# MLA heads in pairs: V as the stationary operand of P times V, two heads in the two column halves

## The chip, the core and the metric

The kernel runs on one core of a Trainium2 chip. Its time is the device time in microseconds (us) of one execution. Each kernel was run several times; the median is given with the lowest and the highest. One execution more was taken with the hardware profiler on, and all rows of a profile come from that one. Engines are named as the profile names them: PE is TensorE's matmuls, PEld its weight loads, DVE VectorE, ACT ScalarE, POOL GpSimd, SP the queue that issues most of the loads.

## The reference: what is computed

One residual block on 512 positions of width 1024, in float32. The attention part, cut to what matters here:

```python
def mla_group(...):                      # 8 heads, 96 wide for q and k, 64 wide for v
    ...
    def one_block(args):
        ...
        logits = jnp.einsum('bhqd,bhkd->bhqk', qb, k_t).astype(jnp.float32) * scale
        logits = jnp.where(allowed[None, None], logits, NEG_INF)
        probs = jax.nn.softmax(logits, axis=-1).astype(v_t.dtype)
        return jnp.einsum('bhqk,bhkd->bhqd', probs, v_t)
    ...

# in reference():
x = x + jnp.concatenate([y_mla, y_diff], axis=-1) @ w_out[i]
x = x + conv_ffn(rms_norm(x, ffn_norm_g[i]), w_gate[i], w_up[i], conv_w[i], conv_b[i], w_down[i])
gate = jax.nn.sigmoid(rms_norm(x, ple_norm_g[i]) @ w_ple_gate[i])
x = x + gate * (p[i] @ w_ple_proj[i])
```

y_diff are four differential heads (two softmaxes each, subtracted, v 128 wide, an RMS norm behind). The mask lets a query see the keys of its own chunk of 64 positions and of all chunks before it.

## The kernel before, in words

Positions lie in four tiles of 128 (t = 0 to 3). Because of the mask a query tile t needs only the keys of tiles 0 to t, so everything of slot t has n = (t+1)·128 columns. Products whose error would matter are made of three matmuls of split operands (`mm3`, lines 157 to 159: high x high, high x low, low x high, in the type fp32r); a split is a cast on ACT (`S.copy`, the high half) and a subtraction on DVE (the low half). Transposes and P times V are plain f32.

In the order of time: the input projections of the latents; the q, k and v of the MLA heads; the eight MLA heads, with the projections of the differential heads (`zd`) as filling; the four differential heads, with the output projection (`o`) as filling; the feed-forward part; the last gate. PE's order is that of the code (`manual_schedule`). For DVE, ACT and POOL the code's order holds up to the `region.__exit__` inside the MLA loop; after it a scheduler orders them when the program is built, within hints such as `tc.issue_after`.

The MLA loop of before runs over 32 slots (h, t). For each:

- `mla_logits(h, t)`, one slot ahead: the logits into a bank `ml` (three matmuls), their row maximum times the query's scale (`nm`, DVE lines 572 and 573), then Exp on ACT into `pm`, with the row sums as a by-product.
- in the slots t < 2 of most heads, `mla_q` or `mla_k` of the next head: four transposes of 96 columns into a bank (`qT`, `kT`) and a split into `st`.
- `pump(n)`: n filling units, of six matmuls of 512 columns each. `FILL_MLA` gives n for t = 0 to 3.
- `probs_T`: t+1 transposes of `pm` into a bank `pT`, and a copy to `pt`, on DVE or ACT by t.
- `mla_pv`, one slot behind: `po[queries, 64] += pt^T · V`, with P as the stationary operand and 64 columns of V moving. After the last slot of a pair of heads one DVE operation scales the bank `mo` by the reciprocal of the sums into `ym` (lines 588 to 590).

The outcome has queries on the partitions. The output projection wants it the other way, so `y_split` transposes each `ym` (four transposes, `yT`) and splits the outcome into `yh` and `yl`. `zd_norm` scales the differential heads' q and k (`zd`) by their RMS on DVE: eleven small steps and four multiplications of 512 columns; it is called at two places in the MLA heads.

Banks of PSUM rotate by tag: two `acc` for filling, three `lg` for logits, two `tp` for transposes (`qT`, `kT`, `pT`), one `ob` for P times V. `pm` has four buffers, `pt` two.

Of the kernel before, what the change touches and what calls it, by code (L numbers as in the profile page):

```python
# [94 lines left out]
def hybrid_block(ctx: ExitStack, tc: tile.TileContext, a: dict, out: bass.AP):  # L95
# [15 lines left out]
    def bank(tag, name):  # L111
        return pp_.tile([P, 512], F32, tag=tag, bufs={"acc": 2, "lg": 3, "tp": 2, "ob": 1}[tag], name=name)
# [7 lines left out]
    def pm_tile(name):  # L120
        return att.tile([P, T], F32, tag="pm", bufs=PM, name=name)
# [10 lines left out]
    def th_tile(name):  # L132
        return wts.tile([P, T], F32R, tag="th", bufs=8, name=name), wts.tile([P, T], F32R, tag="tl", bufs=8, name=name + "l")
# [20 lines left out]
    def mm3(ps, blocks, first=True, last=True, again=False):  # L154
        n = len(blocks)
        for i, (xh, xl, wh, wl) in enumerate(blocks):
            TE.matmul(ps, xh, wh, start=first and i == 0, stop=False, skip_group_check=again)  # L157
            TE.matmul(ps, xh, wl, start=False, stop=False, skip_group_check=again)  # L158
            TE.matmul(ps, xl, wh, start=False, stop=last and i == n - 1, skip_group_check=again)  # L159
# [22 lines left out]
    def split(h_, l_, src, col=None, eng=None):  # L182

        if col is None:
            S.copy(h_, src)  # L185
            return (eng or V).tensor_tensor(l_, src, _f32(h_), op=ALU.subtract)
        else:
            S.activation(h_, src, AF.Identity, scale=col)
            return V.scalar_tensor_tensor(l_, src, col, _f32(h_), op0=ALU.mult, op1=ALU.subtract)
# [342 lines left out]
    pump(FILL_QK)  # L532


    def probs_T(pm, t, name, on_act):

        ps = bank("tp", f"pT{name}")
        n = (t + 1) * P
        for j in range(t + 1):
            TE.transpose(ps[:, tsl[j]], pm[:, tsl[j]], ident)  # L540
# [20 lines left out]

    mla, ymn = {}, []

    def mla_logits(h, t):
        qh_, ql_, kh_, kl_ = QT[h % 2]
        n = (t + 1) * P
        if h % 2 == 0 and t == 0:
            mla["ssum", h // 2] = sm.tile([P, NT, 2], F32, tag="ssum", name="ssum")
        ps = bank("lg", f"ml{h}{t}")
        mm3(ps[:, :n], [(qh_[:100, tsl[t]], ql_[:100, tsl[t]], kh_[:100, :n], kl_[:100, :n])])  # L570
        nm, r = sm.tile([P, 1], F32, tag="nm", bufs=4, name="nm"), rq[:, 0, t, h:h + 1]
        V.reduce_max(nm, ps[:, :n], axis=AX.X, negate=True)  # L572
        mla["nm"] = V.tensor_tensor(nm, nm, r, op=ALU.mult)  # L573
        pm = pm_tile("pm")
        S.activation(pm[:, :n], ps[:, :n], AF.Exp, bias=nm, scale=r, accum_out=mla["ssum", h // 2][:, t, h % 2:h % 2 + 1])  # L575
        mla["pm", h, t] = pm

    def mla_pv(h, t):
        hp, c = divmod(h, 2)
        if c == 0 and t == 0:  # L580
            mla["po"] = bank("ob", f"mo{hp}")
        po, pt = mla["po"], mla.pop(("pt", h, t))
        w = slice(t * P + 64 * c, t * P + 64 * c + 64)
        for j in range(t + 1):
            TE.matmul(po[:, w], pt[:, tsl[j]], kv[j][:, h, 96:], start=j == 0, stop=j == t)  # L585
        if c == 1 and t == NT - 1:
            rcp = sm.tile([P, NT, 2], F32, tag="rcp", name="rcp")
            V.reciprocal(rcp, mla["ssum", hp])
# [26 lines left out]
    def y_split(i, src, col, tag):  # L615

        ps = bank(tag, f"yT{i}")
        for t in range(NT):
            TE.transpose(ps[:, tsl[t]], src[:, tsl[t]], ident)
        yh[i], yl[i] = th_tile(f"yh{i}")  # L620
        df["ysplit"] = split(yh[i], yl[i], ps, col)
# [20 lines left out]
    def wo_units(kq, dqs, nk):  # L642

        for dq in dqs:
            w = wo_w(kq, dq)
            if kq:
                wo2[dq] = w
            for b in (2 * dq, 2 * dq + 1):
                ps = bank("acc", f"o{kq}{b}")
                for k in range(0, nk, 2):  # L650
                    mm3(ps, wo_blocks(4 * kq + k, 4 * kq + k + 2, b, w), k == 0, k == nk - 2)
                    if k == nk - 2:
                        add_x(b, ps)
                    yield

    def diff_T(h, c):
        ps = bank("tp" if h else "acc", f"d{c}T{h}")
# [58 lines left out]
    def load_x():  # L716
# [4 lines left out]
    last_mla = [  # L721
        lambda: diff_T(0, 0),
        lambda: diff_T(0, 1),
        lambda: (y_split(0, ymn[0], None, "acc"), y_split(1, ymn[1], None, "lg"), load_x()),
        lambda: y_split(2, ymn[2], None, "acc"),
    ]
    slots = [(h, t) for h in range(H) for t in range(NT)]
    mla_q(0)
    pump()
    mla_k(0)  # L730
    pump(2)
    mla_logits(0, 0)
    lo(*z1_[1])
    for i, (h, t) in enumerate(slots):
        if i < 2:
            (mla_q, mla_k)[t](1)
        if i + 1 < len(slots):
            mla_logits(*slots[i + 1])
        if i == 4:
            region.__exit__(None, None, None)  # L740
            held = tc.issue_after(mla["nm"].ins)
            held.__enter__()
        if i == 8:
            held.__exit__(None, None, None)
            with tc.issue_after(mla["k"].ins):
                zd_norm(0)
        if 0 < h < H - 1 and t < 2:
            (mla_q, mla_k)[t](h + 1)
        if i == 1:
            lo(*z1_hi(3))  # L750
        if i in (9, 11, 13, 15):
            with tc.issue_after(mla["nm"].ins):
                zw2.append(load_w(a["w_d"][2, len(zw2)], 1024, f"d2{len(zw2)}"))
        if h < H - 1:
            pump(FILL_MLA[t])
        if i == 6:
            bias_strip()
        if h == H - 1:
            if t == 0:
                pump(100)  # L760
                fill.append(wo_units(0, range(4), 4))
            last_mla[t]()
            if t == NT - 1:
                raw = load_raw(a["w_out"][0, 0], 1024, "o00")
                hi_o, lo_o = (wts.tile([P, 1024], F32R, tag=i, bufs=NW, name=f"{i}_o00") for i in ("hi", "lo"))
                S.copy(hi_o, raw)
                with tc.issue_after(df["ysplit"].ins):
                    V.tensor_tensor(lo_o, raw, _f32(hi_o), op=ALU.subtract)
                wo_first[0, 0] = (hi_o, lo_o)
        mla["pt", h, t] = probs_T(mla.pop(("pm", h, t)), t, f"m{h}{t}", t % 2)  # L770
        if i:
            mla_pv(*slots[i - 1])
    diff_logits(0, 0)
    mla_pv(*slots[-1])
    diff_logits(0, 1)
    diff_T(1, 1)
    pump()
    y_split(3, ymn[3], None, "tp")
    for i, (h, t) in enumerate(dslots):
        if i + 2 < len(dslots):  # L780
            diff_logits(*dslots[i + 2])
        pump(FILL_DIFF[h][t])
        df["pt", h, t] = probs_T(df.pop(("pm", h, t)), t, f"d{h}{t}", True)
        if i:
            diff_pv(*dslots[i - 1])
        if h + 1 < DH and t == 0:
            diff_T(h + 1, 0)
        if h and t == 1:
            df["scaling"]()
        if t == 3 and h + 2 < DH:  # L790
            diff_T(h + 2, 1)
        if h and t == 2:
            y_split(4 + h - 1, df["y", h - 1], ocol, "tp")
        if h and t == 3:
            if h == 2:
                fill.append(wo_units(1, range(2), 2))
# [660 lines left out]
```

## Time and profile before

| what | value |
|---|---|
| median of 3 runs | 648.66 us (648.49 to 649.44) |
| the profiled execution's own time | 648.05 us |
| its span, first to last instruction | 646.3 us |
| PE busy | 637.7 us, 99% of the span |
| DVE busy | 480.9 us, 74% |
| ACT busy | 362.3 us, 56% |
| MLA heads in the trace | first logits at 67.5 us, output projection from 161.0 us |
| granted clock of TensorE | 0.999 |

A row of a group of instructions reads: line, engine, operation, output<-inputs, shapes, count, then busy us and mean ns of one, then the idle time of the engine just before them and what ended it. A row of the timeline begins with the start in us and the duration in us; rows of one kind in sequence are merged, with their count behind the x. A matmul's duration holds its way through the array, and the next one starts before its end; so what a matmul takes of PE is read from one start to the next. One f32 matmul (not fp32r, not a transpose) has two records. A row of waits has who waited, for whom, the sum in us, the times and the longest.

### The profile page before, as it was taken

How to read it: one execution, taken by the hardware profiler on the slowest of the kernel's cores; microseconds unless marked ns; L12 is line 12 of the kernel's file. 1: busy time of each engine (PE TensorE's matmuls, PEld its weight loads, DVE VectorE, ACT ScalarE, POOL GpSimd, SP SyncE). 2: the span in 40 equal slices, each digit the busy share in tenths (PEclk: the TensorE clock that was granted, in tenths of full speed). 3: DMA queues.
4: the chain of work that ended last, by engine and by line, in shares of the span. 5: the costliest groups of instructions: out<-in, count | busy, mean ns of one | idle time of the engine just before them, and what ended most of it. 6: DMA issues, size and time to landing. Idle time of an engine off the chain costs nothing.

```text
span 646.3 us, 10248 instructions
## 1 busy us (share of the span) xinstructions
PE 637.7 (99%) x3916; PEld 567.4 (88%) x3916; DVE 480.9 (74%) x870; ACT 362.3 (56%) x630; POOL 56.0 (9%) x92
## 2 busy tenths in 40 slices
PE   9999999999999999999999999999999999999997
PEld 9988888888787887889999999999999999988886
DVE  6889687646988767888876767677767676769844
ACT  7897666556676465657554555455454545537211
POOL 1510040000000121000100000000001000000000
PEclk9999999999999999999999999999999999999999
DMA  8241225130610428636774646464646463541121
GB/s 308 94 164 51 81 82 165 34 125 20 180 37 2 163 87 255 163 66 180 191 216 114 180 115 187 120 195 119 181 114 180 115 180 115 180 131 52 39 89 50
DMA packets 29912, 82.63 MB, mean 128 GB/s; under 512 B 3100, under 2 KB 4124, under 8 KB 29736
## 3 DMA queue, kind: packets, MB, share of 16 engines
q1 hardware_dynamic: 23816, 69.17, 31.7%
q0 software_dynamic: 5616, 12.33, 11.1%
q8 instruction: 31, 0.51, 0.3%
q10 hardware_dynamic: 432, 0.49, 0.2%
q14 instruction: 17, 0.14, 0.1%
HBM read 77.77 MB, written 5.52 MB: 129 GB/s over the span
## 4 chain that ended last, share of the span: by engine, by line
PE 91%; DVE 5%; ACT 3%; issue 1%; ACTq 0%
PE dn L158 6%; PE dn L157 6%; PE dn L159 6%; PE gx L159 4%; PE gx L158 4%; PE gx L157 4%; PE zd L157 3%; PE zd L159 3%; PE zd L158 3%; PE g L157 3%; PE g L158 3%; PE g L159 3%; PE o L157 3%; PE mo L585 2%; PE o L158 2%; PE pg L157 2%
## 5 line engine op out<-in xcount | busy, mean ns | idle before, releaser
L842 DVE TENSOR_TENSOR wSl<-rS,wSh 128x1024 fp32r<-128x1024 f32 x21 | 25.7, 1224 | 44.5 <-ACT wSh L838 44.3
L157 PE MATMUL dn<-ah,hi_dn 128*128 128x512 f32 x144 | 56.2, 391 | 0.0
L158 PE MATMUL dn<-al,hi_dn 128*128 128x512 f32 x144 | 56.2, 391 | 0.0
L159 PE MATMUL dn<-ah,lo_dn 128*128 128x512 f32 x144 | 56.0, 389 | 0.0
L959 POOL DMA_DIRECT2D rS<-in_w_gu x19 | 22.7, 1195 | 250.1 <-DVE cv L1127 100.7
L838 ACT CAST wSh<-rS 128x1024 fp32r<-128x1024 f32 x21 | 22.1, 1050 | 35.9 <-PE gy L158 35.5
L157 PE MATMUL zd<-hi_d,xh 128*128 128x512 f32 x96 | 39.3, 409 | 0.0
L158 PE MATMUL zd<-lo_d,xh 128*128 128x512 f32 x96 | 37.6, 392 | 0.0
L842 DVE TENSOR_TENSOR wTl<-rA,wTh 128x1024 fp32r<-128x1024 f32 x19 | 23.3, 1225 | 15.2 <-ACT wTh L838 14.7
L633 DVE TENSOR_TENSOR x<-x,dn 128x512 f32<-128x512 f32 x44 | 29.9, 679 | 6.1 <-PE dn L159 6.1
L159 PEld LDWEIGHTS dn<-ah,lo_dn 128*128 128x128 f32 x144 | 27.0, 188 | 5.8
L575 ACT ACTIVATE pm<-ml,nm,rq 128x128 f32<-128x128 f32 (+3 forms) x32 | 19.8, 618 | 21.8 <-DVE nm L573 21.7
L157 PEld LDWEIGHTS dn<-ah,hi_dn 128*128 128x128 f32 x144 | 27.1, 188 | 5.2
L158 PEld LDWEIGHTS dn<-al,hi_dn 128*128 128x128 f32 x144 | 27.1, 188 | 4.9
L572 DVE TENSOR_REDUCE nm<-ml 128x1 f32<-128x128 f32 (+3 forms) x32 | 15.6, 488 | 17.9 <-PE ml L159 17.9
L1130 ACT ACTIVATE cv<-cv 128x512 f32<-128x512 f32 x22 | 13.9, 632 | 24.2 <-DVE cv L1127 24.1
L157 PE MATMUL o<-yh,hi_o 128*128 128x512 f32 x64 | 26.9, 421 | 0.5 <-ACT yh L185 0.5
L838 ACT CAST wAh<-rA 128x1024 fp32r<-128x1024 f32 x21 | 22.1, 1052 | 8.4 <-DMA rA<-in_w_gu 8.2
L157 PE MATMUL g<-b2h,wAh 128*128 128x256 f32 (+1 forms) x88 | 26.4, 300 | 0.3 <-ACT g L1083 0.2
L842 DVE TENSOR_TENSOR wAl<-rA,wAh 128x1024 fp32r<-128x1024 f32 x21 | 25.6, 1218 | 1.3 <-ACT wAh L838 1.3
L159 PE MATMUL g<-b2h,wAl 128*128 128x256 f32 (+1 forms) x88 | 26.2, 297 | 0.0
L158 PE MATMUL g<-b2l,wAh 128*128 128x256 f32 (+1 forms) x88 | 26.2, 297 | 0.0
(478 smaller groups left out, 2218.3 us busy)
## 6 DMA issues: line engine op xcount, KB each, us to landing
rA<-in_w_gu SPq DMA_DIRECT2D x22, 512.0 KB, 3.8
rS<-in_w_gu SPq DMA_DIRECT2D x22, 512.0 KB, 3.6
rS<-in_w_gu POOLq DMA_DIRECT2D x19, 512.0 KB, 6.0
raw_dn<-in_w_down SPq DMA_DIRECT2D x18, 512.0 KB, 5.7
raw_d<-in_w_d SPq DMA_DIRECT2D x12, 512.0 KB, 3.4
r<-in_w_gu SPq DMA_DIRECT2D x19, 256.0 KB, 6.0
raw_o<-in_w_out SPq DMA_DIRECT2D x8, 512.0 KB, 3.6
rS_pg<-in_w_pg SPq DMA_DIRECT2D x6, 512.0 KB, 3.8
```

What stands on the lines that cost most here:

```text
L157: TE.matmul(ps, xh, wh, start=first and i == 0, stop=False, skip_group_check=again)
L158: TE.matmul(ps, xh, wl, start=False, stop=False, skip_group_check=again)
L159: TE.matmul(ps, xl, wh, start=False, stop=last and i == n - 1, skip_group_check=again)
L572: V.reduce_max(nm, ps[:, :n], axis=AX.X, negate=True)
L575: S.activation(pm[:, :n], ps[:, :n], AF.Exp, bias=nm, scale=r, accum_out=mla["ssum", h // 2][:, t, h % 2:h % 2 + 1])
L585: TE.matmul(po[:, w], pt[:, tsl[j]], kv[j][:, h, 96:], start=j == 0, stop=j == t)
L633: V.tensor_tensor(xb(b), xb(b), ps, op=ALU.add)
L838: S.copy(h_, src)
L842: V.tensor_tensor(l_, src, _f32(h_), op=ALU.subtract)
L959: nc.gpsimd.dma_start(sums[f].rearrange("p (i c) -> p i c", i=2), a["w_gu"][f][:, :2048].rearrange("p (i c) -> p i c", i=2)[:, :, :512], a ...
L1130: S.activation(cv, cv, AF.Silu)
```

## The change

The loop runs over 16 slots (pair hp, t) in place of 32.

- `mla_logits(hp, t)` makes the logits of both heads, one after the other. For t < 2 both stand in one bank and share one maximum, one product and one `pm` buffer.
- `mla_norm` is new: the reciprocal of the sums and a multiplication of `pm` by it, on DVE, before the transposes. The scaling after P times V is gone.
- `mla_T` transposes both heads' P; for t < 2 into one bank with one copy.
- `mla_pv`: V (64 columns) is the stationary operand, P^T (128 columns) moves. Head 0 of the pair writes partitions 0 to 63 of the bank, head 1 partitions 64 to 127. The outcome has the output's channels on the partitions, as the output projection wants it; so `y_split`'s transposes are gone for the MLA heads (`y_hl` splits at once, the last pair straight from the bank).
- The filling is spread as 1, 2, 2, 2 units over t. The splits of q and k of the next pair stand in t = 2 and t = 3. At the beginning q and k of both heads of pair 0 stand ahead of the first logits.
- At the end, the first output-projection units are ordered so that those that don't need the last pair come first, and the loads of x and the first weight's split move by some slots.

The core of the diff:

```diff
-FILL_MLA = (1, 1, 1, 1)
+FILL_MLA = (1, 2, 2, 2)
...
+    def mla_logits(hp, t):
+        n, one = (t + 1) * P, t < 2
+        r = rq[:, 0, t, 2 * hp:2 * hp + 2]
+        sums = sm.tile([P, 3, 2], F32, tag="sums", bufs=4, name="sums")
+        nm, ssum = sums[:, 0], sums[:, 1]
...
+            mm3(ps[c], [(qh_[:100, tsl[t]], ql_[:100, tsl[t]], kh_[:100, :n], kl_[:100, :n])])
+            if not one:
+                V.reduce_max(nm[:, c:c + 1], ps[c], axis=AX.X, negate=True)
+                mla["nm"] = V.tensor_tensor(nm[:, c:c + 1], nm[:, c:c + 1], r[:, c:c + 1], op=ALU.mult)
+        if one:
+            V.reduce_max(nm, full[:, :2 * n].rearrange("p (c k) -> p c k", c=2), axis=AX.X, negate=True)
+            mla["nm"] = V.tensor_tensor(nm, nm, r, op=ALU.mult)
...
+            S.activation(pm[c], ps[c], AF.Exp, bias=nm[:, c:c + 1], scale=r[:, c:c + 1], accum_out=ssum[:, c:c + 1])
+
+    def mla_norm(hp, t):
+        pm, pmf, sums, one = mla["pm", hp, t]
+        ssum, rcp = sums[:, 1], sums[:, 2]
+        for c in range(2):
+            if not (c and one):
+                w = slice(0, 2) if one else slice(c, c + 1)
+                V.reciprocal(rcp[:, w], ssum[:, w])
+            V.tensor_scalar(pm[c], pm[c], rcp[:, c:c + 1], None, op0=ALU.mult)
...
-            TE.matmul(po[:, w], pt[:, tsl[j]], kv[j][:, h, 96:], start=j == 0, stop=j == t)
...
-            V.tensor_tensor(yn.rearrange("p (t d) -> p t d", d=64), po.rearrange("p (t d) -> p t d", d=64), rcp.rearrange("p t c -> p (t c)").unsqueeze(2).broadcast_to([P, 8, 64]), op=ALU.mult)
+            for c in range(2):
+                TE.matmul(po[64 * c:64 * c + 64, tsl[t]], kv[j][:, 2 * hp + c, 96:], pt[c][:, tsl[j]], start=j == 0, stop=j == t)
+        if t == NT - 1 and hp < H // 2 - 1:
+            yn = tt(f"ym{hp}")
+            S.copy(yn, po)
...
+            steps = [(b, k) for b in (2 * dq, 2 * dq + 1) for k in range(0, nk, 2)]
+            if (kq, dq) == (0, 0):
+                steps.sort(key=lambda s: s[1])
...
+    for hp in range(HP):
+        for t in range(NT):
...
+            if t < NT - 1:
+                mla_logits(hp, t + 1)
+            mla_norm(hp, t)
...
+            if i == 4:
+                held.__exit__(None, None, None)
+                with tc.issue_after(mla["k"].ins):
+                    zd_norm(0)
...
+            if t == 2:
...
+                    mla_q(2 * hp + 2)
+                    mla_k(2 * hp + 2)
+            if t == 3:
+                pump()
+                n -= 1
...
+                    mla_q(2 * hp + 3)
+                    mla_k(2 * hp + 3)
+            pump(n)
...
+            mla_T(hp, t)
+            if i:
+                mla_pv(*divmod(i - 1, NT))
+            if t == 3 and not last:
+                mla_logits(hp + 1, 0)
+    pump(100)
+    fill.append(wo_units(0, range(4), 4))
+    diff_logits(0, 1)
+    diff_T(1, 1)
+    mla_pv(HP - 1, NT - 1)
+    pump()
+    y_hl(3, mla["po"])
```

More of the change, by code (lines that the diff above doesn't have):

```diff
@@ L532, in hybrid_block, with probs_T @@
     pump(FILL_QK)
-    def probs_T(pm, t, name, on_act):
+    def probs_T(pm, n, name, on_act):
         ps = bank("tp", f"pT{name}")
-        n = (t + 1) * P
-        for j in range(t + 1):
-            TE.transpose(ps[:, tsl[j]], pm[:, tsl[j]], ident)
+        for j in range(0, n, P):
+            TE.transpose(ps[:, j:j + P], pm[:, j:j + P], ident)
         pt = pt_tile("pt")
@@ L562, in hybrid_block @@
     mla, ymn = {}, []
-    def mla_logits(h, t):
-        qh_, ql_, kh_, kl_ = QT[h % 2]
-        n = (t + 1) * P
[L567 to L576, printed above, removed]
@@ L581, in mla_pv @@
+    def mla_pv(hp, t):
+        if t == 0:
             mla["po"] = bank("ob", f"mo{hp}")
-        po, pt = mla["po"], mla.pop(("pt", h, t))
-        w = slice(t * P + 64 * c, t * P + 64 * c + 64)
+        po, pt = mla["po"], mla.pop(("pt", hp, t))
         for j in range(t + 1):
[L585 to L588, printed above, removed]
+            for c in range(2):
+                TE.matmul(po[64 * c:64 * c + 64, tsl[t]], kv[j][:, 2 * hp + c, 96:], pt[c][:, tsl[j]], start=j == 0, stop=j == t)
+        if t == NT - 1 and hp < H // 2 - 1:
@@ L719, in load_x, with first_o @@
             nc.sync.dma_start(x_sb[i].rearrange("p (k t) -> p k t", t=T), a["xT"][2 * i * P:(2 * i + 2) * P, :].rearrange("(k p) t -> p k t", p=P))
[L721 to L727, printed above, removed]
+    def first_o():
+        raw = load_raw(a["w_out"][0, 0], 1024, "o00")
+        hi_o, lo_o = (wts.tile([P, 1024], F32R, tag=i, bufs=NW, name=f"{i}_o00") for i in ("hi", "lo"))
+        S.copy(hi_o, raw)
+        with tc.issue_after(df["ysplit"].ins):
+            V.tensor_tensor(lo_o, raw, _f32(hi_o), op=ALU.subtract)
+        wo_first[0, 0] = (hi_o, lo_o)
+    HP = H // 2
     mla_q(0)
@@ L730, in hybrid_block @@
     mla_k(0)
-    pump(2)
+    pump()
+    mla_q(1)
+    pump()
+    mla_k(1)
+    pump()
     mla_logits(0, 0)
     lo(*z1_[1])
[L734 to L772, printed above, removed]
@@ L782, in hybrid_block @@
         pump(FILL_DIFF[h][t])
[L783 removed]
+        df["pt", h, t] = probs_T(df.pop(("pm", h, t)), (t + 1) * P, f"d{h}{t}", True)
         if i:
```

78 lines of the change are left out of this document (63 added, 15 removed).

## The prediction

> **What bounds the kernel now.** I read the page's busy times first, then the table of stretches, then TensorE's waits, and last the timeline of the MLA heads and what follows at once (62 to some 170 us), the only place where instructions change.
>
> ```profile
> PE 637.7 (99%) x3916; PEld 567.4 (88%) x3916; DVE 480.9 (74%) x870; ACT 362.3 (56%) x630; POOL 56.0 (9%) x92
> PE 91%; DVE 5%; ACT 3%; issue 1%; ACTq 0%
> ```
>
> TensorE (PE) is busy throughout and carries 91% of the chain that ended last. So the time is the sum of what PE executes, plus its waits.
>
> ```profile
> 95.00:122.00 27.00, 27.00 (x170) 23.61 (x168) 21.07 (x53) 15.69 (x34) 1.10 (x2) 1.00 0.42 135
> ```
>
> After the length stand the busy times of PE, PEld, DVE, ACT and POOL. In this stretch, the fullest of the heads', PE does not rest and DVE is busy 78%: DVE is the engine with the least room beside it. The granted clock, third from the end, is 1.00.
>
> ```profile
> PE o L158 <- DVE yh3l L186: 0.6, 1, 0.6
> PE pTm L540 <- ACT pm L575: 0.5, 2, 0.3
> PE o L157 <- ACT yh L185: 0.5, 1, 0.5
> PE kT L559 <- DVE st L189: 0.2, 1, 0.2
> ```
>
> These four groups are nearly all that PE waited from 62 to 240 us: two for the last head's output (o), three within the heads.
>
> **The change part by part: PE's own work.** What follows is read from starts in the timeline, since matmuls overlap.
>
> ```profile
> 96.58 0.38 PE L540 MATMUL pTm<-ident,pm 128*128 128x128 f32 x2
> 96.80 0.33 PE L585 MATMUL mo<-kvb,pt 128*128 128x64 f32 x2
> 96.94 0.47 PE L157 MATMUL ml<-st 100*128 100x512 f32 x1
> 97.26 0.39 PE L158 MATMUL ml<-st 100*128 100x512 f32 x1
> 97.48 0.39 PE L159 MATMUL ml<-st 100*128 100x512 f32 x1
> ...
> 99.42 0.56 PE L585 MATMUL mo<-kvb,pt 128*128 128x64 f32 x4
> 99.79 0.31 PE L157 MATMUL ml<-st 100*128 100x128 f32 x1
> ...
> 151.65 1.00 PE L585 MATMUL mo<-kvb,pt 128*128 128x64 f32 x8
> 152.47 0.42 PE L157 MATMUL ml<-st 100*128 100x384 f32 x1
> 152.72 0.33 PE L158 MATMUL ml<-st 100*128 100x384 f32 x1
> 152.90 0.34 PE L159 MATMUL ml<-st 100*128 100x384 f32 x1
> ```
>
> One f32 product is two records. PV (mo) took 0.14 us for 2 records, 0.37 for 4, 0.82 for 8; 6 lie between, at 0.59. A head is 1.92 us, eight heads 15.4. The first logits matmul after it is longer than its fellow: 0.32 against 0.22 at 512 columns, 0.25 against 0.18 at 384. At 0.07 each, 32 blocks of logits paid 2.2. PV in all: 17.6 us.
>
> What column halves cost no row of before shows. The nearest are the differential heads' logits (dl), two row halves:
>
> ```profile
> 184.53 0.38 PE L540 MATMUL pTd<-ident,pmd 128*128 128x128 f32 x2
> 184.75 0.39 PE L692 MATMUL do<-zd,pt 128*128 128x128 f32 x2
> 185.06 0.33 PE L157 MATMUL dl<-st 64*128 64x128 f32 x2
> 185.23 0.28 PE L158 MATMUL dl<-st 64*128 64x128 f32 x2
> 185.34 0.28 PE L159 MATMUL dl<-st 64*128 64x128 f32 x2
> 185.55 0.50 PE L157 MATMUL o<-yh,hi_o 128*128 128x512 f32 x1
> 185.89 0.39 PE L158 MATMUL o<-yh0l,hi_o 128*128 128x512 f32 x1
> ```
>
> Both halves start in one row (x2) and six matmuls take 0.49 us, so halves run side by side. A full-width f32 record with 128 moving columns is 0.11 (two transposes in 0.22); two of PV's (do) took 0.31 up to dl, 0.09 too much: entering costs 0.09, a slower second step 0.06 (0.17 against 0.11), leaving 0.10 (0.21 against 0.11), and the next full matmul's load 0.11 (0.34 against 0.23). That is 0.36 a visit. The new PV has 16 visits: 5.8 us. Its two chains of 2(t+1) records for t = 0 to 3 are 20 records of 0.11 a pair, 2.2 us, 8.8 for four pairs, if the halves overlap; 17.6 if they do not. I take overlap, by dl, the only halves in the trace: 14.6 us, so -3.0 (+5.8 without it). The Trainium skill, TensorEngine Tiling (Array Packing), Key Properties, says that tiles execute loads and matmuls in parallel, but that a change of tiling mode drains the engine; for columns no run here shows either, and by it the sum would be this -3.0.
>
> The order of the built program, at slot (pair 1, t = 0), shows the new block on PE. Before, at head 0, t = 1 (pT is the transposed P, ml logits):
>
> ```order
> L540 MATMUL pTm_926<-ident,pm 128x128 x2
> L585 MATMUL mo_931<-kvb,pt 128x64
> L157 MATMUL ml_933<-st 128x512
> L158 MATMUL ml_933<-st 128x512
> L159 MATMUL ml_933<-st 128x512
> L157 MATMUL zd_835<-hi_d_759,xh_167 128x512
> ```
>
> Now, pair 1, t = 0:
>
> ```order
> L539 MATMUL pTm_1192<-ident,pm 128x128 x2
> L620 MATMUL mo_972<-pt,kvb 64x128 x8
> L157 MATMUL ml_1208<-st 128x384
> L158 MATMUL ml_1208<-st 128x384
> L159 MATMUL ml_1208<-st 128x384
> L157 MATMUL ml_1214<-st 128x384
> ```
>
> Two heads' logits follow one PV; 64x128 is the half-width product.
>
> The transposes of the MLA outputs go:
>
> ```profile
> 154.64 1.04 PE L619 MATMUL yT<-ident,ym 128*128 128x128 f32 x8
> ```
>
> There are sixteen of these full transposes (eight here, eight in two other places), 0.11 us each as the two of P that stand ahead of do above: -1.75. With them goes the chain at the end, PV, scaling, transpose, split, output projection; the split now reads PV's bank and two units of projection stand ahead of its user. Its two waits (0.6 and 0.5) go, and with the 0.7 of pTm and kT, which I count anew below, that is -1.8. P's transposes, the logits and the filling units (six matmuls of 512 columns of zd or o) stay in number, though one more unit now stands ahead of the first logits and a pair has seven in place of eight; the order of loads on SP's queue and of POOL's work is the same as before. Three copies of PV's bank on ACT take the place of DVE's scalings; a filling unit (six steps of 0.23, as the 0.22 from 97.26 to 97.48, or 1.4 us) covers one, and without that cover it would cost PE about 0.7.
>
> **The change part by part: DVE and the new waits.** Scaling P puts 32 multiplications and 24 reciprocals on DVE, between Exp and the transposes.
>
> ```profile
> 88.97 0.28 DVE L572 TENSOR_REDUCE nm<-ml 128x1 f32<-128x128 f32 x1
> 89.16 0.68 DVE L403 TENSOR_TENSOR zd<-zd,rd 128x512 f32<-128x512 f32 x1
> 89.76 0.15 DVE L573 TENSOR_TENSOR nm<-nm,rq 128x1 f32<-128x1 f32 x1
> 89.83 1.29 DVE L403 TENSOR_TENSOR zd<-zd,rd 128x512 f32<-128x512 f32 x2
> 91.04 0.20 DVE L588 RECIPROCAL rcp<-ssum 128x8 f32<-128x8 f32 x1
> ```
>
> From start to start a step is shorter than its duration by some 0.08 (zd: 0.60 for 0.68). Here the scaling of zd (zd<-zd,rd) already stands between a maximum (88.97) and its product (89.76), and PE did not wait, since the transposes of that head came later. For the new multiplication:
>
> ```profile
> L170 DVE TENSOR_SCALAR nr<-nr 128x512 f32<-128x512 f32 x1 | 0.7, 692 | 1.5 <-PE nr L1361 1.5
> L572 DVE TENSOR_REDUCE nm<-ml 128x1 f32<-128x512 f32 x8 | 5.5, 688 | 4.0 <-PE ml L159 4.0
> L572 DVE TENSOR_REDUCE nm<-ml 128x1 f32<-128x256 f32 x8 | 3.4, 421 | 8.9 <-PE ml L159 8.9
> L189 DVE SCALAR_TENSOR_TENSOR st<-qT,qcol,st 96x512 fp32r<-96x512 f32 x8 | 5.9, 743 | 1.7 <-ACT st L188 1.6
> L305 DVE TENSOR_TENSOR lo_d<-raw_d,hi_d 128x1024 fp32r<-128x1024 f32 x8 | 9.8, 1228 | 3.0 <-ACT hi_d L301 3.0
> L575 ACT ACTIVATE pm<-ml,nm,rq 128x128 f32<-128x128 f32 x8 | 3.7, 456 | 7.3 <-DVE nm L573 7.3
> L575 ACT ACTIVATION_READ_ACCUMULATOR pm<-ml,nm,rq 128x1 f32 x32 | 6.2, 194 | 0.0
> ```
>
> It lies between 0.15 (a product of one column) and 0.69 at 512; I take the nearest, the same operation: 0.69, 0.29 at 128. The Trainium skill, VectorE: DVE Perf Modes, The perf-mode tier table, runs fp32 tensor_scalar at double speed when it reads SBUF; L170 reads PSUM, so nothing here shows it, and by it the outcome would be that of rival (b).
>
> Slot t = 0 is the tight one. Before, one head's logits and its transposes had two filling units, a PV and more between them. Now only the next logits (six of 0.11 to 0.12, 0.7) and one unit (1.4) stand there, 2.1 us. DVE's and ACT's chain without anything between: maximum 0.42, product 0.15, two Exp with read-out 2 x 0.55, reciprocal 0.16, two multiplications 0.5, and 0.2 of matmul drain: 2.5 us, so 0.5 of wait. In the pair where zd is scaled the order on DVE is, before:
>
> ```order
> L403 TENSOR_TENSOR zd_789<-zd_789,rd 128x512
> L545 COPY pt<-pTm_1104 128x384
> L572 TENSOR_REDUCE nm<-ml_1113 128x1
> L403 TENSOR_TENSOR zd_800<-zd_800,rd 128x512
> L573 TENSOR_TENSOR nm<-nm,rq 128x1
> L403 TENSOR_TENSOR zd_811<-zd_811,rd 128x512
> L403 TENSOR_TENSOR zd_822<-zd_822,rd 128x512
> ```
>
> and now:
>
> ```order
> L403 TENSOR_TENSOR zd_789<-zd_789,rd 128x512
> L582 TENSOR_REDUCE sums<-ml_1134 128x2
> L403 TENSOR_TENSOR zd_800<-zd_800,rd 128x512
> L583 TENSOR_TENSOR sums<-sums,rq 128x2
> L582 TENSOR_REDUCE sums<-ml_1147 128x2
> L403 TENSOR_TENSOR zd_811<-zd_811,rd 128x512
> L583 TENSOR_TENSOR sums<-sums,rq 128x2
> L600 RECIPROCAL sums<-sums 128x2
> L403 TENSOR_TENSOR zd_822<-zd_822,rd 128x512
> L601 TENSOR_SCALAR pm<-pm,sums 128x128 x2
> ```
>
> All four zd scalings now stand ahead of the P scaling for which PE's next transposes wait. From the copy of the last P (0.60): two small 0.33, zd 4 x 0.60, maxima 0.33 and 0.60, products and reciprocal 0.21, multiplications 0.5: 5.0 us. PE meanwhile runs four transposes 0.44, PV 0.9, logits 0.75 and 0.7, one unit 1.4: 4.2, less 0.3 of latency; and DVE starts some 1.2 late, after nine small steps of the norm (0.15 to 0.2 each, like the product). So 2.3 us of wait. Pair 2 has the second such norm, ahead of the copy rather than behind: 1.9 by the same count. Pair 0: a low half (1.23) stands between the maxima, 1.1. Pair 3: 0.5. Together 5.8.
>
> The other slots, counted alike: pair 0, t = 1, a low half waits for its cast, then 1.2; t = 2, the transposes' second bank waits for the splits of q and k (0.74 each, k's behind the Exp of 512 columns on ACT), 0.4, 1.2 (three low halves stand there) and 0.5; t = 3, 0.7. That is 3.6, new waits in all 9.4 us, each behind a PE instruction with all of PE queued after it. Bounds: 2.0 (only the bare chain, four times 0.5) and 14 (each slot half as much again).
>
> Sum: -3.0 - 1.75 - 1.8 + 9.4 = +2.85 us. The profiled execution took 648.05 (span 646.3, 1.75 around it), 0.6 under the median 648.66; 648.05 + 2.85 = 650.9, as a median 651.5. I say 651.1.
>
> **Rivals.** (a) Faster: PE falls back in the first long wait of a pair, and DVE is level with it from there, so that one wait of 1.0 and the bare 0.5 in four slots are left. At 3.0 it is 648.66 - 6.55 + 3.0 = 645.1; it decides below 5.2. For it: DVE idles 22% even in its fullest stretch. Against: the order above. (b) Even: the multiplication of P takes the middle of its bounds, 0.42 at 512 columns and 0.22 at 128. Slot t = 0 then gains 0.14 in each pair, t = 1 of pair 0 0.3, and t = 2 0.5 in three pairs, 2.4 in all: waits of 7.0 and 649.0. It decides from 7.9 down to 5.2. For it: the bounds are far apart. Against: the one row of that operation. (c) The halves don't overlap: PV +8.8, and a later PE waits some 3 less: 651.1 + 5.8 = 656.9. Against it, dl's pairs. A DVE bound is none: the 32 multiplications (0.49 on the mean) and 24 reciprocals (0.16) are 19.5 us, less 6 for the merged maxima and products and the old scaling, so 3.4 a pair on some 24; DVE in the fullest stretch goes from 78% to about 92%, under full. The waits are of order, not of load.
>
> **How the numbers follow.** My forecast has 0.46 (own range 650.0 to 655.0), (a) 0.29, (b) 0.16, (c) 0.09. About 0.2% (1.3 us) is what a measurement here can tell from no change. Faster is (a), same (b), slower the forecast and (c), 0.55. The range leaves out the far ends of (a) and most of (c): 644.0 to 656.0.
>
> **What would show it.** In the profile after: PV (L620) in two interleaved rows; waits of pTm (L539) on DVE's pm (L601), longest at t = 0 of pairs 1 and 2; no yT<-ym; no wait of o on yh3. If those waits sum under 5 us the forecast is wrong; if L620's records of one head follow the other's, (c) holds.

## The result: slightly slower, by the waits that were forecast

The changed kernel took 652.97 us (median of 4 executions, 651.15 to 653.39) against 648.96 us of the kernel before on the same chip (4 executions): a ratio of 1.0056, 95% interval [1.0035, 1.0078]. In a later session it took 652.46 us, 1.0057 [1.0043, 1.0070]. The forecast was 651.1 us, with 650.9 as the sum for the profiled execution; the profiled execution of after took 651.15 us, with a span of 649.4.

The page of after answers to the page of before line by line: the busy times, the chain, the stretch 95 to 122 us.

```profile
PE 634.6 (98%) x3900; PEld 556.3 (86%) x3900; DVE 489.2 (75%) x898; ACT 361.4 (56%) x629; POOL 57.5 (9%) x92
PE 84%; DVE 10%; ACT 4%; issue 1%; DMA 1%; ACTq 0%
```
```profile
95.00:122.00 27.00, 22.85 (x148) 17.85 (x146) 23.77 (x63) 15.76 (x36) 1.11 (x2) 1.00 0.46 146
165.00:185.00 20.00, 20.00 (x130) 15.61 (x127) 15.03 (x48) 13.08 (x36) 0.00 (x0) 1.00 0.16 52
```

PE has 3 us less work, and the span is 3 us longer. DVE's share of the chain went from 5% to 10%: PE now stands behind it. In the stretch that PE filled before (27.00 of 27) it is busy for 22.85, with DVE at 23.77. From 165 to 185 us, where the output projection waited for `yh3` before (PE busy for 19.26 of 20 us), PE does not rest.

PE's waits from 62 to 240 us:

```profile
PE pTm L539 <- DVE pm L601: 4.9, 4, 2.1
PE zd L158 <- DVE lo_d L305: 0.9, 1, 0.9
PE pTm L539 <- DVE st L186: 0.7, 1, 0.7
PE mo L620 <- DVE pt L544: 0.5, 1, 0.5
PE pTm L539 <- DVE st L189: 0.2, 1, 0.2
PE d1T L699 <- ACT pt L542: 0.2, 1, 0.2
```

The first row is the P scaling (line 601), for which the transposes of P wait. The two longest stand where the order of DVE put them, at t = 0 of pair 1 and of pair 2. DVE's timeline ahead of the first, and PE behind it:

```profile
95.26 0.68 DVE L403 TENSOR_TENSOR zd<-zd,rd 128x512 f32<-128x512 f32 x1
95.86 0.15 DVE L583 TENSOR_TENSOR sums<-sums,rq 128x2 f32<-128x2 f32 x1
95.93 0.68 DVE L582 TENSOR_REDUCE sums<-ml 128x2 f32<-128x512 f32 x1
96.53 0.68 DVE L403 TENSOR_TENSOR zd<-zd,rd 128x512 f32<-128x512 f32 x1
97.13 0.15 DVE L583 TENSOR_TENSOR sums<-sums,rq 128x2 f32<-128x2 f32 x1
97.20 0.16 DVE L600 RECIPROCAL sums<-sums 128x2 f32<-128x2 f32 x1
97.27 0.67 DVE L403 TENSOR_TENSOR zd<-zd,rd 128x512 f32<-128x512 f32 x1
97.86 0.48 DVE L601 TENSOR_SCALAR pm<-pm,sums 128x128 f32<-128x128 f32 x2
...
98.29 0.43 PE L539 MATMUL pTm<-ident,pm 128*128 128x128 f32 x2 [2.09 <-DVE pm L601]
98.65 1.09 PE L620 MATMUL mo<-pt,kvb 128*64 128x128 f32 x16
99.68 0.44 PE L157 MATMUL ml<-st 100*128 100x384 f32 x1
```

The reader sees DVE without a pause, with the scalings of `zd` (0.60 from start to start) between the maxima, the products and the multiplication at 97.86 for which PE stands still. DVE is not overloaded; it does in this moment what nobody waits for.

The matmuls of P times V, grouped, before and after (160 records each; the duration overlaps, the busy time counts overlap once):

```profile
L585 PE MATMUL mo<-kvb,pt 128*128 128x64 f32 x160 | 21.6, 266 | 0.0
```
```profile
L620 PE MATMUL mo<-pt,kvb 128*64 128x128 f32 x160 | 12.3, 283 | 0.5 <-DVE pt L544 0.5
```

One record has twice the moving columns, yet all of them cover 12.3 us instead of 21.6, because two run at a time. The changed kernel's records start in couples 6 to 8 ns apart, and behind the second couple, which comes after 0.16 us, the couples follow each other at 0.109 us.

### The profile page after: what moved, and what is told of

Its sections match the earlier page's. It is cut to its first block, busy times and chain, and to the rows that moved or that the text cites. A ratio compares the mean times of both kernels' runs of the same rounds, so it can differ in the third digit from the quotient of the medians.

```text
span 649.4 us, 10234 instructions
## 1 busy us (share of the span) xinstructions
PE 634.6 (98%) x3900; PEld 556.3 (86%) x3900; DVE 489.2 (75%) x898; ACT 361.4 (56%) x629; POOL 57.5 (9%) x92
## 4 chain that ended last, share of the span: by engine, by line
PE 84%; DVE 10%; ACT 4%; issue 1%; DMA 1%; ACTq 0%
PE dn L157 6%; PE dn L158 6%; PE dn L159 6%; PE gx L159 4%; PE gx L158 4%; PE gx L157 4%; PE g L157 3%; PE g L158 3%; PE g L159 3%; PE o L157 3%; PE o L159 2%; PE pg L159 2%; PE pg L158 2%; PE o L158 2%; PE pg L157 2%; PE zd L157 2%
## 5 line engine op out<-in xcount | busy, mean ns | idle before, releaser
L718 ACT ACTIVATE pmd<-pmd,nmd 128x128 f32<-128x128 f32 (+3 forms) x32 | 17.9, 561 | 15.9 <-DVE nmd L717 15.9
L590 ACT ACTIVATE pm<-ml,sums,rq 128x128 f32<-128x128 f32 (+3 forms) x32 | 19.5, 616 | 12.6 <-DVE sums L583 7.5
```

The source lines that it names most:

```text
L590: S.activation(pm[c], ps[c], AF.Exp, bias=nm[:, c:c + 1], scale=r[:, c:c + 1], accum_out=ssum[:, c:c + 1])
L718: S.activation(pm[:, :n], pm[:, :n], AF.Exp, bias=nm, scale=-1.0, accum_out=s0 if m == 0 else s1)
```

## The experiments

All that the change touches lies between the first transposes of q (62 to 64 us) and the first product of the differential heads (`do`, 163 to 182 us). I call this the stage. Its length is read in each profiled execution from those two starts (62.4 and 171.4 us in the kernel before, 62.6 and 173.9 in the changed one), which leaves out what varies ahead of it and behind it. Between them every kernel runs the same matmuls in the same number; only the kernel before has the sixteen transposes of `ym` besides, and V as the moving operand. A visit is one stay of PE in the column halves, from full-width work to full-width work. The clock column counts executions whose mean granted clock was 0.997 or less. Where the profiled execution was one of them (changed again, no scaling, one half, sixteen visits, wait longer), the stage holds that loss too.

| kernel | median us | ratio to before, 95% | stage, us | low clock |
|---|---|---|---|---|
| before | 648.75 to 649.12 | | 109.0 | 0 of 55 |
| changed | 652.97 | 1.0056 [1.0035, 1.0078] | 111.3 | 3 of 4 |
| changed, again | 652.46 | 1.0057 [1.0043, 1.0070] | 112.8 | 5 of 6 |
| zd moved | 646.95 | 0.9971 [0.9962, 0.9981] | 107.0 | 0 of 12 |
| no scaling | 651.19 | 1.0032 [1.0018, 1.0046] | 111.7 | 8 of 12 |
| heads in sequence | 653.84 | 1.0078 [1.0065, 1.0092] | 113.7 | 2 of 6 |
| one half | 658.66 | 1.0142 [1.0123, 1.0161] | 118.8 | 4 of 5 |
| twelve visits, PV ahead | 644.97 | 0.9938 [0.9926, 0.9951] | 105.1 | 0 of 5 |
| sixteen visits, PV ahead | 646.36 | 0.9953 [0.9936, 0.9969] | 107.3 | 3 of 7 |
| wait longer | 653.95 | 1.0082 [1.0070, 1.0095] | 115.2 | 4 of 5 |
| combined, twelve visits | 640.24 | 0.9872 [0.9860, 0.9885] | 100.4 | 0 of 4 |
| combined, eight visits | 641.13 | 0.9885 [0.9872, 0.9898] | 101.1 | 0 of 4 |
| combined, sixteen visits | 641.96 | 0.9895 [0.9880, 0.9910] | 102.0 | 0 of 5 |

### Are the waits a matter of order or of load?

The first experiment moves the eight zd scalings behind later P scalings, one at a time, and changes nothing in amount (the low halves of pair 1 are tied to the same place, so that they don't slip in front):

```diff
+    ZD_AT = {5: (0, 0), 6: (0, 1), 7: (0, 2), 8: (0, 3), 9: (1, 0), 10: (1, 1), 11: (1, 2), 12: (1, 3)}
...
+            if i in ZD_AT:
+                with tc.issue_after(mla["sc"].ins):     # the last P scaling
+                    zd_scale(*ZD_AT[i])
...
-                with tc.issue_after(mla["nm"].ins):
+                with tc.issue_after(mla["sc"].ins):
                     zw2.append(load_w(a["w_d"][2, t], 1024, f"d2{t}"))
```

> Only the eight scalings of zd (0.68 us each on DVE) are moved: out of the slots t = 0 of pairs 1 and 2, one each behind the P scaling of the slots from pair 1, t = 1 to pair 3, t = 0. DVE's work is the same. Theory A (the new waits are set by what stands ahead of the P scaling in DVE's order): the waits of pTm at t = 0 of pairs 1 and 2, 2.25 and 1.88 us, fall to 0.5 or less each, and at most 0.5 us comes back elsewhere: 649.7 us, between 649.0 and 650.5. Theory B (DVE has too much work in pairs 1 and 2, wherever it stands): the waits come back in the next slots, 652 to 653.4 us.

Measured: 646.95 us. The waits of the transposes on the P scaling:

```profile
PE pTm L539 <- DVE pm L601: 1.7, 4, 0.8
PE zd L158 <- DVE lo_d L305: 0.9, 1, 0.9
```
```profile
95.00:122.00 27.00, 26.38 (x179) 21.25 (x178) 25.36 (x68) 17.36 (x40) 1.10 (x2) 1.00 0.50 154
```

The first row fell from 4.9 to 1.7, the longest from 2.1 to 0.8. The stretch 95 to 122 now has PE busy for 26.38 us, and DVE for more than before the move, 25.36, with little of PE's time lost to it. So it was the order; theory B is out. The stage lost 4.3 us. By starts 3.2 of them went at t = 0 of pairs 1 and 2 (2.25 to 0.5 and 1.88 to 0.4), as A expected, and 1.0 more at t = 2 and 3 of pair 1. The median lost 6.0, which is below A's range (649.0 to 650.5): A had left out that 1.0 and the 1.9 that the clock costs in the changed kernel's median (below).

The second leaves the scaling away altogether (the call of `mla_norm` goes).

> Leaves out the reciprocals and the multiplications of P, so P is not divided by its sum; Exp is followed by the transposes at once. Theory A (order on DVE): the waits of pTm at t = 0 shrink to what Exp sets: 2.25 to 1.1, 1.88 to 1.0, 0.42 to 0, pair 0 t = 1 0.95 to 0.4, t = 3 0.41 to 0; the wait on a low half (1.0) and those at the end (0.28, 0.54) stay. Together 3.4 us less: 649.6 us, between 648.5 and 651. Theory B (the P scaling sets all the waits): they go altogether, 9 us less, 644 us.

Measured: 651.19 us. In the executions without a low clock it was 648.65 to 649.18, some 2.1 us under the changed kernel's 650.81 and 651.15; A expected 3.4 less, B 9. By the median it lies just above A's range (648.5 to 651), but eight of its twelve executions had a low clock. The waits at t = 0 shrank (the one of 2.25 to 0.67 and 0.33 more between the two transposes, from start to start; A had 1.1), but a new one of 2.3 us came up in the last slot of pair 1:

```profile
113.92 2.48 DVE L403 TENSOR_TENSOR zd<-zd,rd 128x512 f32<-128x512 f32 x4
116.33 0.68 DVE L186 TENSOR_TENSOR st<-kT,st 96x512 fp32r<-96x512 f32 x1
117.06 0.33 PE L539 MATMUL pTm<-ident,pm 128*128 128x128 f32 x1 [2.30 <-DVE st L186]
```

With the scaling gone the order of DVE came out otherwise, and four zd scalings stand ahead of the split of kT, whose bank the transposes need. Even without a single multiplication of P, four of the same eight instructions hold PE for 2.3 us. A's size was off, because it took the rest of the order as given.

### Do the two column halves run side by side?

```diff
-        for j in range(t + 1):
-            for c in range(2):
+        for c in range(2):
+            for j in range(t + 1):
                 TE.matmul(po[64 * c:64 * c + 64, tsl[t]], kv[j][:, 2 * hp + c, 96:], pt[c][:, tsl[j]], ...)
```

> PV runs all blocks of one head, then all of the other, so that neighbouring matmuls stand in the same column half. Theory A (the halves run side by side only when neighbours in PE's order stand in different halves): of 20 pairs of records in a pair of heads 18 come apart, 18 x 4 x 0.109 us = 7.8 us more PE time, of which some 2.5 us only take the place of the waits at t = 0 that follow: 652.97 + 5.3 = 658.3 us, between 656.5 and 661. Theory B (each half has its own queue and runs ahead): within 0.7 us of 653.0 us.

Measured: 653.84 us, and a profiled span of 651.9, 2.5 more than after at the same clock. Neither theory fits well. By the median it is just above B's bound; A's 658.3 is far off. The records say why. From the first record to the next matmul a visit with t = 0, 1, 2, 3 took 0.37, 0.59, 0.81, 1.02 us interleaved, and 0.37, 0.59, 1.07, 1.51 in sequence. With t = 3 the first four records of head 0 run alone, then head 1's start beside the rest of head 0's, and head 1's last ones run alone. So PE goes on in its order up to some four records ahead, if those stand in the other half: short visits lose nothing, long ones lose 0.27 and 0.49.

The next kernel tells whether this needs the halves. It is the one in sequence, but in pairs 0 to 2 both heads go to partitions 0 to 63, so that the second head's output takes the place of the first's (the copy of the bank to `ym` then reads these partitions twice, which the lines below don't show):

```diff
+                u = 64 * c * (hp == HP - 1)
-                TE.matmul(po[64 * c:64 * c + 64, tsl[t]], ...
+                TE.matmul(po[u:u + 64, tsl[t]], ...
```

> As the kernel with the heads in sequence, but in pairs 0 to 2 both heads write to the same column half (so the second head's output takes the place of the first's). There a visit of PV took 0.37, 0.60, 1.07 and 1.51 us for t = 0 to 3, and 0.37, 0.59, 0.81 and 1.02 with the heads interleaved. Theory A (it is the two halves that let PE run ahead, by some four records): in one half all 4(t+1) records follow each other at 0.109, a visit takes 0.59, 1.02, 1.46 and 1.90 us, 2.18 us more a pair than interleaved, 6.5 in three pairs; 1.7 of that takes the place of waits at t = 0: 655.9 us, between 655 and 657. Theory B (PE runs ahead in any case): visits as with the heads in sequence, 653.8 us.

Measured: visits of 0.58, 1.02, 1.45 and 1.89 us in pairs 0 to 2, as theory A has them (but for one of 3.04 at half clock), and 0.37 to 1.51 in pair 3, which kept its two halves. A visit of t = 3, 1.09 in the changed kernel above, in sequence and in one half:

```profile
99.25 1.58 PE L620 MATMUL mo<-pt,kvb 128*64 128x128 f32 x16
```
```profile
127.34 1.96 PE L621 MATMUL mo<-pt,kvb 128*64 128x128 f32 x16
```

The median was 658.66 us, above A's 655 to 657; the one execution with a clock of 1.0 took 656.14, which is A's 655.9. Theory A's times hold, and the rest is the clock again. The edit puts both heads not only into one half but also to the same addresses of the bank; no run parts these two.

### What a visit costs, and where PV stands

```diff
-            mla_T(hp, t)
-            if i:
-                mla_pv(*divmod(i - 1, NT))
+            if i and t != 1:
+                if t == 2:
+                    mla_pv(hp, 0)
+                mla_pv(*divmod(i - 1, NT))
+            mla_T(hp, t)
```

> PV of t = 0 and t = 1 stand together (12 visits of PE to the column halves in place of 16), and each PV stands ahead of the next transposes of P, no longer behind them. Theory A (a visit costs 0.36 us beside its records, and the waits of pTm are what DVE lacks in time): 4 x 0.36 = 1.4 us less for the visits, and PV (0.7 to 1.1 us) now covers part of each wait at t = 0 and t = 2 to 3: 1.1 + 0.9 + 0.4 + 0.6 = 3.0 us less: 648.6 us, between 647.3 and 650. Theory B (the cost of a visit lies in its records, or the PV now waits for the copies of P as long as the transposes waited for P): 651 to 653 us.

Measured: 644.97 us, 3.6 under A's 648.6. Of this 1.9 is the clock. In the stage it was 6.2 us: 1.4 by A's price of the visits, and 3.6 of waits by starts (4.6 went; 0.7 is new at t = 1 of pair 1, 0.3 at a q); 1.2 I cannot assign. The longest wait is now 1.3 us, with PV ahead of it:

```profile
119.09 1.09 PE L620 MATMUL mo<-pt,kvb 128*64 128x128 f32 x16
121.46 0.43 PE L539 MATMUL pTm<-ident,pm 128*128 128x128 f32 x2 [1.28 <-DVE pm L601]
```

To part the two edits, PV ahead of the transposes, but in 16 visits (only the order of `mla_pv` and `mla_T` is swapped):

> Each PV ahead of the next transposes of P as in the twelve-visit kernel, but in 16 visits. Theory A (a visit costs 0.36 us beside its records): 644.97 + 4 x 0.36 = 646.4 us, between 645.6 and 647.2. Theory B (a visit costs nothing beside its records, all of that kernel's gain is the place of PV): 645.0 us. Theory C (the place brings nothing, all the gain is in the visits): 651 us or more.

Measured: 646.36 us, A's number, but not for A's reason. Four of seven executions had a clock of 0.998 or more and took 644.76, 644.98, 645.14 and 646.56, the twelve-visit kernel's time; the other three had 0.996 and 646.36 to 647.83. So without the clock B holds here: the PV ahead of the transposes of t = 1 covered there what the visits cost: the wait of 0.7 us at t = 1 of pair 1 is 0.2, and the one in pair 0 is 0.5 shorter. The price of a visit had to be tried where hardly a wait is left, below.

### Why the median lies above the profiled execution

> The changed kernel once more, unaltered, in a session with the others, for its mean granted clock in many executions: three of the first four had 0.996 and 652.7 to 653.4 us, the profiled one 0.999 and 651.15 us. Theory A (the 2.2 us of PE's rest at t = 0 of pair 1, or the 1.9 of pair 2, sometimes make the clock fall to half for some 5 us, as the trace of the kernel without scaling shows after a rest of 2.3 us): two groups, 651.0 us at a clock of 0.998 or more and 653.0 us at 0.997 or less, with more in the second. Theory B (the clock falls by chance, whatever the waits): no tie of clock and time, and the kernel before falls as often.

Measured: 650.81 us at a clock of 0.999, and 652.24 to 653.76 in five executions at 0.996. With the first four executions: 650.98 us on the mean of two, 652.92 on the mean of eight. This time the profiled execution was one of the second kind, and shows the place. PE behind the wait at t = 0 of pair 1:

```profile
98.49 0.44 PE L539 MATMUL pTm<-ident,pm 128*128 128x128 f32 x2 [2.08 <-DVE pm L601]
98.86 1.23 PE L620 MATMUL mo<-pt,kvb 128*64 128x128 f32 x16
100.02 0.69 PE L157 MATMUL ml<-st 100*128 100x384 f32 x1
100.51 0.52 PE L158 MATMUL ml<-st 100*128 100x384 f32 x1
...
102.11 0.63 PE L157 MATMUL zd<-hi_d,xh 128*128 128x512 f32 x1
102.53 0.63 PE L158 MATMUL zd<-lo_d,xh 128*128 128x512 f32 x1
102.96 0.46 PE L159 MATMUL zd<-hi_d,xh4l 128*128 128x512 f32 x1
103.26 0.40 PE L157 MATMUL zd<-hi_d,xh 128*128 128x512 f32 x1
103.50 0.39 PE L158 MATMUL zd<-lo_d,xh 128*128 128x512 f32 x1
```

and the granted clock (third from the end) in stretches of 5 us:

```profile
95.00:100.00 5.00, 2.92 (x25) 1.94 (x23) 4.75 (x13) 3.02 (x9) 0.00 (x0) 0.97 0.63 176
100.00:105.00 5.00, 5.00 (x19) 4.45 (x18) 3.89 (x12) 2.01 (x5) 0.87 (x1) 0.69 0.74 252
105.00:110.00 5.00, 5.00 (x32) 3.93 (x31) 3.06 (x7) 3.16 (x6) 0.30 (x1) 1.00 0.47 168
```

From about 100 to 103 us the products of 512 columns start 0.43 us apart, behind that 0.23: half the clock for some 3 us. 0.31 of 5 us and 0.03 of 5 make 1.7 us lost, close to the difference of the two groups (1.9). Theory A holds: the kernel before never had it.

The wait made longer:

```diff
-            V.reduce_max(nm, full[:, :2 * n]...
+            for _ in range(3 if (hp, t) == (1, 1) else 1): V.reduce_max(nm, full[:, :2 * n]...
```

> The changed kernel with the maximum of pair 1's slot t = 1 taken three times over (same outcome), ahead of the P scaling that PE waits for: 1.2 us more on DVE, so that PE's rest there is 3.4 us instead of 2.2. Theory A (a rest of this length halves the clock for some 5 us): nearly every execution has a mean clock of 0.996 or less, and 651.15 + 1.2 + 2.3 = 654.7 us, between 653.8 and 655.5. Theory B (the clock falls by chance): 652.4 us where the clock stays at 0.999, and as many such executions as of the unaltered kernel.

Measured: 653.95 us, with a clock of 0.994 to 0.997 in four of five executions, and 652.69 at 1.0 in the fifth. The profiled rest, and the first transposes at half clock behind it (0.66 for 0.43):

```profile
99.87 0.66 PE L539 MATMUL pTm<-ident,pm 128*128 128x128 f32 x2 [3.21 <-DVE sums L583]
```

A's time is in its range, and B's 652.4 is what the one undisturbed execution took; but a longer rest does not make the fall certain, and its share (4 of 5) can't be told from the 8 of 10 of the unaltered kernel.

### What is left when the order is mended

Three edits together: zd moved, twelve visits with PV ahead, and in pair 0 the low half of the second weight made right after the first k, with the third weight's cast ahead of the first logits.

```diff
     mla_k(0)
+    lo(*z1_[1])
     pump()
     mla_q(1)
     pump()
     mla_k(1)
+    z1_.append(z1_hi(3))
     pump()
     mla_logits(0, 0)
-    lo(*z1_[1])
...
-                lo(*z1_hi(3))
+                lo(*z1_[2])
```

> The changed kernel with three edits together: the eight zd scalings moved, PV in twelve visits ahead of the transposes, and the two low halves of pair 0 made earlier. Theory A (order on DVE sets what is left): of the twelve-visit kernel's 644.97 us go the waits at t = 0 of pairs 1 and 2 (1.25 and 1.3), those of pair 0 (1.0 on the low half, 0.95 at t = 1) and 0.5 at t = 1 of pair 1: 640.0 us, between 639 and 642. Theory B (DVE's load is the bound by now, it is busy 24.9 of 27 us in pair 1): the waits come back, 643 to 645 us.

Measured: 640.24 us, faster than the changed kernel and, by 1.28% [1.15, 1.40], than the kernel before. PE's waits and the former trouble stretch:

```profile
PE pTm L539 <- DVE pm L601: 0.5, 2, 0.3
PE kT L558 <- ACT pt L542: 0.4, 1, 0.4
PE qT L551 <- DVE st L189: 0.2, 1, 0.2
```
```profile
95.00:122.00 27.00, 26.61 (x177) 21.93 (x175) 25.46 (x71) 16.75 (x38) 1.10 (x2) 1.00 0.40 125
```

Of the 7.4 us in the list of after 1.1 is left, though DVE is busier in this stretch (25.46 of 27) than where it held PE. Theory B (load) is out.

The same with 16 visits, and with 8 (for which P's copies have four buffers and another tag of buffers one less):

> The combined kernel (zd scalings moved, low halves earlier, PV ahead of the transposes), but with PV of t = 0 and t = 1 apart again: 16 visits in place of 12. Hardly a wait is left in the combined kernel, so a visit should show its price here. Theory A (0.36 us a visit beside its records): 640.24 + 1.44 = 641.7 us, between 641.0 and 642.3. Theory B (nothing, or a PV that stands ahead of the transposes of t = 1 covers as much of a wait as its visit costs): 640.2 us, within 0.5.

> As the combined kernel with twelve visits, but PV of t = 2 and t = 3 together too, ahead of the next pair's first transposes: 8 visits. Theory A (a visit costs 0.36 us beside its records): 4 x 0.36 = 1.4 us under the combined kernel with twelve visits: 638.6 us if that comes to 640.0, less where the longer PV covers a wait. Theory B (a visit costs nothing beside its records): the same time within 0.5 us.

Measured: 641.96 us with 16 visits, 1.7 more than with 12; A expected 1.4, so a visit has its price where no wait takes it over. The intervals of the two ratios overlap by a little; the stages, 102.0 and 100.4 at a clock of 1.0 both, say the same in one execution each. With 8 visits it was 641.13, which neither theory has (638.6, or 640.2 within 0.5). Its stage is 101.1 us, 0.7 longer than with twelve: a wait of 0.7 stands now ahead of the differential heads' transposes, and others of 0.3. What four visits less are worth there stays open, since the new waits stand for them.

## Why the prediction was right, point by point

- **PV, -3.0 forecast.** Held. The sixteen visits took 4 x (0.37 + 0.59 + 0.81 + 1.02) = 11.2 us, entering them 0.09 each (0.20 for 0.11), the slower first logits behind them 0.05 to 0.11, together some 14.1; 14.6 was forecast, from the row halves of `dl`. Beside its records (8.7 us) a visit costs 0.34 on the mean, where 0.36 was taken. Rival (c), halves that don't overlap, fell; the one-half kernel shows its price, 2.2 us a pair. The Trainium skill, TensorEngine Tiling (Array Packing), Key Properties, says that tiles run in parallel and that a change of mode drains the engine; the 6 to 8 ns between the halves' starts agree with the first, and the 0.34 us of a visit go with the second, though no trace here shows the drain itself.
- **Transposes and removed waits, -1.75 and -1.8.** No `yT<-ym` is left, and no wait of `o` on `yh3`. By starts, PE's own work and the waits that went make up for the stage so: 109.0 - 2.5 (the long gaps of before, beyond the usual step) + 9.4 (those of after) - x = 111.3, so x = 4.6; the forecast had 3.0 + 1.75. Read one by one, PV (17.6 to 14.1) and the transposes make 5.25; the 0.6 between them stays open. The waits that went are 2.5 by starts, where 1.8 was forecast.
- **New waits, +9.4.** The sum of the long gaps of after, each less the usual step, is 9.4 us, the forecast's number. But its terms did not all come so. By slot:

  | pair, t | 0, 0 | 0, 1 | 0, 2 | 0, 3 | 1, 0 | 1, 2 | 2, 0 | 2, 2 | 3, 0 |
  |---|---|---|---|---|---|---|---|---|---|
  | forecast, us | 1.1 | 1.2 | 0.4 | 0.7 | 2.3 | 1.2 | 1.9 | 0.5 | 0.5 |
  | measured, us | 1.0 | 0.95 | 0 | 0.4 | 2.25 | 0.85 | 1.9 | 0.25 | 0.4 |

  The terms as listed make 9.8 (the 3.6 for the slots behind t = 0 was added wrongly, it should have been 4.0); measured they make 8.0. At t = 0 of pair 0 PE waited for the low half itself, in the filling unit, and not for the maximum behind it; at t = 2 of pair 1 for the split of k. The rest is made up by gaps that the forecast did not have: 0.3 at the second q, 0.3 at t = 3 of pair 1, and 0.3 and 0.5 at the end of the last pair, where PV and the next transposes wait for the last copies of P. (The bare chain at t = 0, 2.5 against 2.1, makes 0.4 and not the 0.5 that the forecast wrote; pair 3 measured that.) So the sum's exactness is partly luck. Its two largest terms are not: they came as worked out from the order of DVE, and moving the zd scalings took them away.
- **The multiplication of P, 0.69 us at 512 columns: wrong.**

```profile
L601 DVE TENSOR_SCALAR pm<-pm,sums 128x512 f32<-128x512 f32 x8 | 3.7, 480 | 0.1
L601 DVE TENSOR_SCALAR pm<-pm,sums 128x384 f32<-128x384 f32 x8 | 3.2, 416 | 0.1
L601 DVE TENSOR_SCALAR pm<-pm,sums 128x256 f32<-128x256 f32 x8 | 2.6, 349 | 0.1
L601 DVE TENSOR_SCALAR pm<-pm,sums 128x128 f32<-128x128 f32 x8 | 1.9, 283 | 0.1
```

  (480 - 283) / 384 = 0.51 ns a column, half of the maximum's 1.04 ((688 - 421) / 256, from the rows of before). The rule of the Trainium skill that the forecast weighed and left aside (VectorE: DVE Perf Modes, The perf-mode tier table: fp32 tensor_scalar from SBUF at double speed) is the right one, and the nearest row, which read PSUM and took 0.69, misled. It did little harm, because the tight slots multiply 128 columns, where 0.28 was measured and 0.29 taken. For the same reason rival (b) did not come, though the price at 512 columns, 0.48, lies nearer to its 0.42 than to 0.69: it had 0.22 at 128.
- **Rival (a), PE falls back only once a pair: fell.** DVE did not level out after a first wait, and the long gaps stand in every pair. Its 645 us is what the twelve-visit kernel reached by another order.
- **What the sum did not have: the clock.** The sum was for an execution at full clock, 650.9, and such executions took 650.81 and 651.15. Eight of ten took 1.9 us more, because PE's rest let the clock fall. The median is above the forecast by just this.
- **Outside the stage** the profiled execution of after took 0.8 us more than that of before (0.2 ahead of it, 0.6 behind), where no instruction changed. In the second profiled execution the part from the start of the last `do` to PE's last instruction was as long as in before (421.3 us, against 421.7 in the first), so this is how executions vary. Within the stage the change was +2.3 us, less than the sum's +2.85; that the profiled execution came within 0.3 of the forecast owes something to these 0.8.

## What to carry to other kernels

When work is moved to an engine that is three quarters busy, don't ask only whether it fits: write down what stands in that engine's order ahead of the result at the slot with the least cover, and place work that nobody waits for behind that result; here this was worth 4.3 us in the stage, of the some 7 that the change takes off PE there (4.6 of work, 2.5 of waits). Two matmuls in the column halves overlap fully if they alternate, and each switch between halves and full width costs about a third of a microsecond on PE, so gather them where no wait would be exposed by it. A rest of PE costs its length and, from about 1.7 us here, the risk of some 2 to 3 us more.

## What the runs showed of the hardware

- **The clock falls in, or within 1.5 us behind, rests of PE of 1.65 to 3.2 us.** Kernels whose longest rest in the profiled execution was 1.3 us or less (before, zd moved, twelve visits, the three combined) had no execution of 85 with a mean clock under 0.998; only five of these executions, those with twelve visits, are of a kernel whose longest rest is over 0.9 us. With a longest rest of 1.65 us it was 3 of 7, with 1.83 2 of 6, with 2.1 8 of 10, with 2.3 8 of 12, with 2.6 and 3.2 4 of 5 each. Where a trace shows the fall, matmuls start at double distance: the clock records have 3.4 us at half clock in three of the five traces (changed again, one half, sixteen visits) and 6.8 to 6.9 in two (no scaling, wait longer). The loss follows: medians of the low and the full executions are 1.7 us apart with sixteen visits, 2.6 without scaling. The Trainium skill, TensorE: Matmul & The Clock Gate, section What's actually happening, has half rate after an idle window of some 3.4 us, in windows that run free of the program. That the fall comes in some executions only, and lasts 3.4 us or twice that, agrees with windows; rests of 1.65 us that suffice do not agree with a whole window of idleness, and the measurement decides. The rest of 1.65 us, in the kernel with sixteen visits and PV ahead, and a product behind it:

```profile
119.81 0.44 PE L539 MATMUL pTm<-ident,pm 128*128 128x128 f32 x2 [1.65 <-DVE pm L601]
...
121.55 0.63 PE L158 MATMUL zd<-lo_d,xh 128*128 128x512 f32 x1
```

- **PE runs ahead in its order across column halves**, by some four records of 0.109 us, so that even two heads in sequence overlap fully where a head has four records or fewer (t = 0 and 1). With both heads at the same addresses of one half no records overlap.
